# Output projection as seven half-size products instead of eight, in a hybrid encoder layer on one Trainium2 core

## The chip, the core and the metric

The kernel runs on one core of one Trainium2 chip. The metric is the device time of one execution in microseconds (us): the median of several runs of the whole program. The engines are called PE (TensorE, matrix products), PEld (its weight loads), DVE (VectorE), ACT (ScalarE), POOL (GpSimd) and SP (SyncE, which here only issues DMAs). POOL issues DMAs too, the stores above all.

## The reference, cut to what matters

One layer of an encoder on 1024 tokens of width 1024, in float32. Around the change it computes

```
merged = sigmoid(gate_a) * a_out + sigmoid(gate_b) * b_out
x  = x + gt1 * (merged @ w_o)                    # the output projection, w_o is 1024 x 1024
h2 = rmsnorm(x, norm2_g) * (1 + sc2) + sh2
f_gate, f_up = split(h2 @ w_ffn_in, 2)           # 2 x 2816 columns
x  = x + gt2 * ((silu(f_gate) * f_up) @ w_ffn_out)
```

`gt1`, `sc2` and `sh2` come from `mod = silu(c) @ w_ada + b_ada`, one column of 128 numbers at a time (48 columns).

## The kernel before, in words

Channels lie on the 128 partitions, tokens on the free axis; the tokens are worked in two halves of 512 ("half 0" and "half 1"). Every float32 operand is split into a high part (rounded to fp32r by ACT: `A.copy`) and a low part (`source - high`, on DVE: `V.tensor_tensor`), and a product is three matmuls: high x high, high x low, low x high (`mm3`, line 161; `multiply`, line 1286). Weights come as **units** of 128x1024: a DMA into a `raw` tile, ACT's cast to `wh`, DVE's difference to `wl` (`unit`, line 153). The three tags `raw`, `wh` and `wl` have three buffers each (pool `wpool`), and a load, a cast or a difference waits until the user of the unit three places earlier is done with that buffer. Tiles with the tag `mid` (128x2048) have eight buffers.

The program runs through these stages: `half(0)` and then `half(1)` (line 568), each with the input projections of query, key and value, the attention, the spatial gating, and at its end a loop over eight row blocks `d` that projects both branches (`w_ab`); `gate_products` (line 1295), the gates of row blocks 2 to 7 for both halves, already as seven products by Strassen's form; `out_projection(0)` and `out_projection(1)` (line 1395); then the feed-forward part (from line 1466), again by Strassen's form.

`out_projection(hf)` goes over eight row blocks `d` of the output. Each has one unit of `w_o`, 24 matmuls of 128x512 (eight `k`, three each) into one PSUM bank, then on DVE `x1 = bank * gt1 + x`, on ACT the square, on DVE the running sum of squares, and a store of `x1` to DRAM (`x1d`). The unit of `d + 2` is prepared beside `d`. In half 0, eight columns of `mod` (`ada_next`) and the split of half 1's merged rows run beside it; in half 1, the second norm of half 0 (`second_norm`: one DVE instruction, one of ACT, one of DVE for each of eight row blocks) does.

The loop over `d` at the end of `half(0)` (from line 1070) prepares the unit of `w_ab` for `d + 2`, computes the sum of squares of half 1's tokens, four columns of `mod` (`ada_next(2)` at `d` 2 and 3: each a raw load of 512 KB and a DVE instruction over 128x1024), and from `d` 5 on half 1's normalised input. In the first stage of `half(1)`, `ada_load` at `k` 0 to 5 loads twelve more columns, two to a `mid` tile, and `ada_late` uses them.

What sets the order: inside these stages `in_order[0]` is true, and then every DVE, ACT and PE instruction stays in the order of the program text (`Engine`, line 69), each engine working through its list and waiting at the head of it. Outside them a scheduler places instructions when the program is built. Loads on SP's queue (`load`) always keep program order, so that one which waits for a buffer holds all that come behind it. `in_order` is true in the loop at the end of `half(0)` in part only, and in `gate_products` throughout.

Of the kernel before, what the change touches and what calls it, by code (L numbers as in the profile page):

```python
# [8 lines left out]
F32 = mybir.dt.float32  # L9
F32R = mybir.dt.float32r  # L10
# [6 lines left out]
P = 128  # L17
# [24 lines left out]
def kernel(  # L42
# [58 lines left out]
    def nm(s):  # L101
        n_names[0] += 1
        return f"{s}_{n_names[0]}"
# [44 lines left out]
    def raw_unit(src):  # L148
        r = wpool.tile([P, UNIT], F32, tag="raw", name=nm("raw"))
        load(r, src)  # L150
        return r
# [94 lines left out]
    wS = dram.tile([NP, P, 4 * HALF], F32, tag="wS", name="wS")  # L246
    tA = dram.tile([NP, P, 4 * HALF], F32, tag="tA", name="tA")
    tB = dram.tile([NP, P, 4 * HALF], F32, tag="tB", name="tB")


    apool_ctx = ExitStack()
# [250 lines left out]
    def open_ffn():  # L502

        apool_ctx.close()
        fp = ffn_ctx.enter_context(pool("ffn"))
        fps.append(fp)
        for part in range(2):
            t = fp.tile([P, 2048], F32R, tag=f"b22{'hl'[part]}", name=nm("first"))
            firsts[part] = t

    def first_unit(i):

        r = raw_unit(w_gate[EARLY - 2 + i])
        h, l = (firsts[p][:, i * UNIT : (i + 1) * UNIT] for p in range(2))
        A.copy(h, r)
        V.tensor_tensor(l, r, h.bitcast(F32), op=ALU.subtract)
        return h, l

    halo_v = {}
    x1B = []  # L520
# [8 lines left out]
    def ada_late(r, col, row):  # L529

        V.scalar_tensor_tensor(out=r, in0=r, scalar=1.0, in1=row, op0=ALU.mult, op1=ALU.mult,
                               accum_out=acc_mod[:, col : col + 1])
        if col % 4 == 3:
            b = slice(col - 3, col + 1)
            if col < SH2:
                V.scalar_tensor_tensor(out=mod[:, b], in0=acc_mod[:, b], scalar=0.5, in1=base[:, b],
                                       op0=ALU.mult, op1=ALU.add)
            elif SC2 <= col < GT2:
                V.tensor_tensor(mod[:, b], acc_mod[:, b], g2c[:, col - SC2 - 3 : col - SC2 + 1], op=ALU.mult)
                V.tensor_tensor(mod[:, b], mod[:, b], base[:, b], op=ALU.add)  # L540
            else:
                V.tensor_tensor(mod[:, b], acc_mod[:, b], bada[:, b], op=ALU.add)
# [25 lines left out]
    def half(hf):  # L568
# [103 lines left out]
        for k in range(KT):  # L672
# [96 lines left out]
            if hf == 1:  # L769

                if k in (0, 2, 4):
                    wq_raw = raw_unit(w_q[k // 2 + 1])
                if k == 2:
                    wk_raw = raw_unit(w_kv[1])
                if k == 4:
                    wk = unit(None, V, wk_raw)
                if k in (1, 3, 5):
                    wq_next = unit(None, V, wq_raw)
                for _ in range((0, 0, 2, 2, 2, 3, 3, 0)[k]):
                    ada_late(*ada_loaded.pop(0), silu_c)  # L780
                if k < 6:
                    ada_load()
            sts = [(hH[k // 4][:, k % 4, t * P : (t + 1) * P], hL[k // 4][:, k % 4, t * P : (t + 1) * P])
# [286 lines left out]
        for d in range(KT):  # L1070
# [62 lines left out]
                    in_order[0] = False  # L1133
            if d == 4:
                h_next.extend([[hid(), hid()], [hid(), hid()]])
            if d in (2, 3):
                ada_next(2)
            if d > 4:
                for k in ((0, 1), (2, 3, 4), (5, 6, 7))[d - 5]:
                    xk = xs[k // 4][:, k % 4, :]  # L1140
                    hi, lo = (t[k // 4][:, k % 4, :] for t in h_next)
                    modulate(xk, rb, k, SC1, SH1, hi, lo, xk)
                    store(hd[1, k * P : (k + 1) * P, :], xk)
# [91 lines left out]
    def run_tokens(n):  # L1235
        for _ in range(n):
            if tokens:
                tokens.pop(0)()
# [56 lines left out]
    def gate_products(hH, hL):  # L1295
# [21 lines left out]
        for d in GD:  # L1317
            banks = {}
            for i, (u, part, t, b, first) in enumerate(STEPS):
# [30 lines left out]
                elif i == 6:  # L1350
# [4 lines left out]
                        split(merged[0][1][:, 3, :], mH[1][:, 3, :], mL[1][:, 3, :])  # L1355
                    gate_low(d + 1, 1)
                run_tokens((0, 4, 4, 4, 0, 0, 0)[i])
                if d == KT - 1:
                    if i == 2:
                        mH, mL = [hid(), hid()], [hid(), hid()]  # L1360
                    if i in (2, 3, 5):
                        for k in ((0, 1), (2, 3, 4), (), (5, 6))[i - 2]:
                            split(merged[0][k // 4][:, k % 4, :], mH[k // 4][:, k % 4, :],
                                  mL[k // 4][:, k % 4, :])
                    if i == 4:
                        wo_units.append(unit(w_o[0]))
                    if i == 6:
                        wo_units.append(unit(w_o[1]))
                if (d, i) == (GD[0], 5):
                    for hf in range(2):  # L1370
                        merged.append([midt(F32, 4), midt(F32, 4)])
# [12 lines left out]
                elif i == 6:  # L1384
# [2 lines left out]
                    merge(c21, ps[1, 1])  # L1387
                    V.tensor_tensor(merged[1][d // 4][:, d % 4, :], s, c21, op=ALU.add)
                    ps = load_p(d + 1)
        in_order[0] = False  # L1390
        return (mH, mL), merged[1]

    wo_units = []

    def out_projection(hf, m, m_next):

        mH, mL = m
        if hf == 1:
            h2[0] = [[hid(), hid()], [hid(), hid()]]
            dst = h2[0]  # L1400
            x1B.extend([midt(F32, 4), midt(F32, 4)])
            h2m.extend([midt(F32, 4), midt(F32, 4)])
        else:
            out = [[midt(F32R, 4), midt(F32R, 4)] for _ in range(2)]
            cond = midt(F32, 2)[:, 0, :]
            load(cond, cd)
        ss = ss_tile()[:, :HALF]

        def second_norm(k):
            xk = stream("hs")  # L1410
            load(xk, x1d[k * P : (k + 1) * P, :HALF])
            hi, lo = (t[k // 4][:, k % 4, :] for t in dst)
            modulate(xk, rb, k, SC2, SH2, hi, lo, h2m[k // 4][:, k % 4, :])

        for d in range(KT):
            wo = wo_units.pop(0)
            if d + 2 < KT:
                wo_units.append(unit(w_o[d + 2]))
            elif hf == 0:
                wo_units.append(unit(w_o[d + 2 - KT]))  # L1420
            elif d == KT - 1:
                raw1 = raw_unit(w_gate[1])
                raw2.append(raw_unit(w_gate[2]))
            if hf == 1 and d == 6:
                early.append(unit(w_gate[0], V))
            in_order[0] = hf == 0 and d < 2 or hf == 1 and d > 5
            if hf == 1 and d in (2, 5):
                early.append(first_unit(d // 3))
            xr = stream("xs")
            load(xr, x_rows(hf, d))  # L1430
            pw = mm_bank()
            for k in range(KT):
                kc = slice(k * P, (k + 1) * P)
                mm3(pw, (wo[0][:, kc], wo[1][:, kc]),
                    (mH[k // 4][:, k % 4, :], mL[k // 4][:, k % 4, :]), k == 0, k == KT - 1)
            if hf == 1:
                if d == 0:
                    col_rstd(sums[0], NT, rcol[2])
                elif d == 1:
                    rb = spread(rcol[2], NT)  # L1440
                for k in ((), (0,), (1, 2), (3,), (4, 5), (6,), (7,), ())[d]:
                    second_norm(k)
            else:
                ada_next((0, 0, 2, 2, 2, 2, 0, 0)[d], cond)
                split(m_next[d // 4][:, d % 4, :], out[0][d // 4][:, d % 4, :],
                      out[1][d // 4][:, d % 4, :])
            x1 = tmp() if hf == 0 else x1B[d // 4][:, d % 4, :]
            V.scalar_tensor_tensor(out=x1, in0=pw, scalar=mod[:, GT1 + d : GT1 + d + 1], in1=xr,
                                   op0=ALU.mult, op1=ALU.add)
            sumsq(x1, d == 0, ss)  # L1450
            store(x1d[d * P : (d + 1) * P, hf * HALF : (hf + 1) * HALF], x1)
            if hf == 1 and d == KT - 1:
                early.append(unit(None, V, raw1))
        in_order[0] = False
        sums.append(ss)
        if hf == 0:
            return out

    half(0)
    m = gate_products(*half(1))  # L1460
    m = out_projection(0, *m)
    out_projection(1, m, None)

    fp = fps[0]

    B11, B21 = ((h2[0][0][q], h2[0][1][q]) for q in range(2))
    T1, T2 = ((fpt(f"{n}h"), fpt(f"{n}l")) for n in ("tt1", "tt2"))


    RG, RU, U = {}, {}, {}
# [172 lines left out]
    def chain_rest():  # L1645
        def new_block(name):
            BLK[name] = (midt(F32R, 4), midt(F32R, 4))

        BLK["B22"] = (fpt("b22h"), fpt("b22l"))
        for name, q in (("T3", 0), ("T4", 1)):  # L1650
            for k in range(4):
                chain.append(lambda k=k, q=q, name=name: (k or new_block(name), t34_sum(q, k)))
                if k:
                    chain.append(lambda k=k, q=q, name=name:
                                 low(h2m[q][:, k - 1, :], BLK[name], k - 1))
            chain.append(lambda q=q, name=name: low(h2m[q][:, 3, :], BLK[name], 3))
# [342 lines left out]
```

## Time and profile before

| what | value |
| --- | --- |
| device time, median of 3 runs (lowest, highest) | 1227.25 us (1225.9, 1227.33) |
| span of the profiled execution, first to last instruction | 1224.2 us |
| device time outside that span, median less span | 3.05 us |
| PE busy in the span, matmuls | 1217.5 us (99%), 5701 |
| DVE, ACT, POOL busy | 897.4, 578.5, 148.7 us |
| granted TensorE clock | 1.000 |

The profiled execution's own device time is not listed; its span and the 3.05 us stand for it. A busy time is the union of an engine's instructions, which overlap a little where they follow each other; a row of the time line gives start, duration, engine, operation and tiles, and in brackets the idle time before it with what ended it.

### The profile page before, as it was taken

What the parts mean: (1) busy time and instruction counts of PE and PEld (TensorE: products, weight loads), DVE (VectorE), ACT (ScalarE), POOL (GpSimd) and SP (SyncE); (2) the same over time, 40 slices, a digit from 0 to 9 for tenths busy, and PEclk for the clock granted to TensorE, in tenths of its full rate; (3) what the DMA queues carried; (4) which work ended last, traced back from release to release, by engine and by line L of the source; (5) the groups of instructions that cost most, each with busy time, mean ns of one, the idle gap of its engine ahead of it and who ended that gap; (6) DMA issues with size and microseconds to landing.
All of it is one profiled execution on the core that took longest, in us unless ns stands there. A gap on an engine that the chain in (4) does not pass through costs nothing.

```text
span 1224.2 us, 15630 instructions
## 1 busy us (share of the span) xinstructions
PE 1217.5 (99%) x5701; PEld 1016.0 (83%) x5701; DVE 897.4 (73%) x1449; ACT 578.5 (47%) x944; POOL 148.7 (12%) x178
## 2 busy tenths in 40 slices
PE   9999999999999999999999999999999999999998
PEld 7888888888888888888888888888888888888887
DVE  9988877788878766877797766675676766765646
ACT  5667855367855434634453233333333334433341
POOL 0124323114331000011000001000000000010001
PEclk9999999999999999999999999999999999999999
DMA  9721179521176333597413446455555439995552
GB/s 366 283 86 52 35 241 361 223 86 53 35 276 222 120 104 121 198 322 264 154 52 120 172 155 224 172 176 202 189 189 187 167 153 367 393 364 190 189 172 104
DMA packets 75937, 230.79 MB, mean 189 GB/s; under 512 B 8658, under 2 KB 8914, under 8 KB 71124
## 3 DMA queue, kind: packets, MB, share of 16 engines
q1 hardware_dynamic: 61444, 161.62, 38.3%
q0 software_dynamic: 14416, 68.17, 14.9%
q8 instruction: 45, 0.74, 0.3%
q14 instruction: 32, 0.26, 0.1%
HBM read 174.70 MB, written 55.05 MB: 188 GB/s over the span
## 4 chain that ended last, share of the span: by engine, by line
PE 92%; DMA 4%; DVE 2%; issue 1%; ACT 1%; SPq 0%; POOL 0%; POOLq 0%; DVEq 0%; ACTq 0%
PE mm L79 48%; PE at L79 45%; DMA wS<-wo 1%; DMA mid<-in_w_ada_dram 1%; DMA raw<-in_w_q_dram 1%; DMA wo<-in_w_out_dram 1%; DMA mid<-in_xA_dram 0%; DVE mid L79 0%; ACT mid L79 0%; DVE wl L79 0%; DVE ws L79 0%; ACT wh L79 0%; DVE lb L79 0%; DVE hid L79 0%; DVE wo L79 0%
## 5 line engine op out<-in xcount | busy, mean ns | idle before, releaser
L79 PE MATMUL mm<-mid,wh 128*128 128x512 f32 x704 | 217.4, 390 | 0.0
L79 ACT CAST wh<-raw 128x1024 fp32r<-128x1024 f32 (+1 forms) x151 | 154.3, 1023 | 120.9 <-PE mm L79 45.6
L79 DVE TENSOR_TENSOR wl<-raw,wh 128x1024 fp32r<-128x1024 f32 (+1 forms) x137 | 161.5, 1183 | 62.1 <-ACT wh L79 61.1
L79 PEld LDWEIGHTS mm<-mid,wh 128*128 128x128 f32 x704 | 131.7, 188 | 27.1
L79 PE MATMUL mm<-mid,wl 128*128 128x512 f32 x352 | 137.0, 389 | 0.0
L79 PE MATMUL mm<-wh,h 128*128 128x512 f32 x384 | 124.6, 396 | 0.2 <-ACT h L79 0.2
L79 PE MATMUL mm<-h,wh 128*128 128x512 f32 x400 | 123.9, 391 | 0.0
L79 PEld LDWEIGHTS mm<-h,wh 128*128 128x128 f32 x400 | 74.6, 188 | 15.4
L79 PE MATMUL at<-h,wh 128*128 128x512 f32 x272 | 84.0, 390 | 0.0
L79 PEld LDWEIGHTS mm<-wh,h 128*128 128x128 f32 x384 | 70.8, 188 | 13.8 <-ACT h L79 0.4
L79 DVE TENSOR_TENSOR wl<-ws,wh 128x1024 fp32r<-128x1024 f32 (+1 forms) x54 | 60.7, 1125 | 24.5 <-ACT wh L79 24.5
L79 PE MATMUL mm<-h,wl 128*128 128x512 f32 x200 | 77.9, 389 | 0.0
L79 PEld LDWEIGHTS mm<-mid,wl 128*128 128x128 f32 x352 | 66.1, 188 | 13.8
L79 ACT CAST wh<-ws 128x1024 fp32r<-128x1024 f32 (+1 forms) x54 | 52.5, 973 | 42.3 <-DVE ws L79 27.4
L79 PE MATMUL mm<-wl,h 128*128 128x512 f32 x192 | 71.2, 391 | 0.0
L79 ACT ACTIVATE t<-t 128x512 f32<-128x512 f32 x53 | 32.8, 630 | 72.0 <-DVE t L79 71.9
L79 PEld LDWEIGHTS at<-h,wh 128*128 128x128 f32 x272 | 50.9, 188 | 10.5
L79 DVE TENSOR_TENSOR ol<-raw,oh 128x1024 fp32r<-128x1024 f32 x30 | 36.5, 1223 | 30.0 <-ACT oh L79 28.4
L79 ACT ACTIVATE xs<-xs 128x512 f32<-128x512 f32 x21 | 13.3, 633 | 94.0 <-DVE xs L79 94.0
L79 PE MATMUL at<-h,wl 128*128 128x512 f32 x136 | 53.1, 390 | 0.3 <-DVE wl L79 0.3
L79 PE MATMUL at<-wl,wh 128*128 128x512 f32 (+1 forms) x136 | 52.7, 388 | 0.0
L79 PE MATMUL at<-wh 128*128 128x512 f32 (+1 forms) x136 | 52.7, 387 | 0.0
(275 smaller groups left out, 2729.5 us busy)
## 6 DMA issues: line engine op xcount, KB each, us to landing
raw<-in_w_gate_dram SPq DMA_DIRECT2D x28, 512.0 KB, 3.8
tA<-hid POOLq DMA_DIRECT2D x11, 1024.0 KB, 4.6
tB<-hid POOLq DMA_DIRECT2D x11, 1024.0 KB, 5.0
wo<-in_w_out_dram POOLq DMA_DIRECT2D x22, 512.0 KB, 5.9
wS<-wo POOLq DMA_DIRECT2D x11, 1024.0 KB, 5.2
raw<-wS SPq DMA_DIRECT2D x44, 256.0 KB, 3.5
raw<-tB SPq DMA_DIRECT2D x44, 256.0 KB, 4.8
mid<-in_w_ada_dram SPq DMA_DIRECT2D x20, 512.0 KB, 9.8
```

The lines of the kernel that those rows point to most:

```text
L79: ins = f(*args, **kw)
```

## The change

The output projection of both halves is made by one level of Strassen's form (in Winograd's variant): row blocks are taken in four pairs, each pair needs seven products of 12 matmuls (four `k`, three each) instead of eight (two row blocks, two halves, two halves of `k`).

- **Weights.** Four of the seven products use sums of quarters of `w_o`. Those sums are made from `w_o` by `merged_sums(p)`: two loads of 512 KB into a `mid` tile, four DVE additions of 128x512, one store of 1 MB to a new DRAM tensor `sO`. Pairs 0 to 2 are made in the loop at the end of `half(0)`, pair 3 in the first stage of `half(1)`. The projection loads them back as units ("A", "C"); "0" and "B" are units of `w_o` itself. There are 14 units instead of 16.
- **Tokens.** The blocks T1 to T4 are sums of the merged rows of both halves: T1's four subtractions run in `gate_products` at `d` 4 and 5, its splits at `d` 7 (steps 4 and 5); T2, T3, T4 and the split of B22 are in a list `todo`, of which `run(3)` takes three entries after each product.
- **Order.** First the eight products of half 0's even row blocks (M1, M2), then for two pairs at a time T2, T3, T4, then T1 and B22. Each product is followed by its DVE addition into the rows it belongs to (`accumulate`, 28 instead of 16). The M1 bank stays open for T2, T3 and T4: each of these products continues in the bank that the addition before it has read.
- **Columns of `mod`.** The eight columns that `out_projection(0)` computed are moved ahead: `ada_next(2)` now runs at `d` 1 to 4 of `half(0)`, `ada_load` also at `d` 6 and 7, and `half(1)` uses sixteen instead of twelve.
- The second norm of half 0 is now in place in `h2m` and runs beside the last eight products; two tiles of the feed-forward part change places (`tt2`, `b22`).

The core of the diff:

```diff
+    sO = dram.tile([KT // 2, P, 4 * HALF], F32, tag="sO", name="sO")
...
+    def merged_sums(p):
+        t = mid.tile([P, 2048], F32, tag="mid", name=nm("wo"))
+        for i in range(2):
+            load(t[:, i * UNIT : (i + 1) * UNIT], w_o[2 * p + i])
+        a11, a12, a21, a22 = (t[:, i * HALF : (i + 1) * HALF] for i in range(4))
+        ops = [(a22, a21, a22), (a21, a11, a21), (a11, a22, a11), (a12, a11, a12)]
+        def one(n):
+            out, a, b = ops[n]
+            V.tensor_tensor(out, a, b, op=ALU.add)
+            if n == 3:
+                store(sO[p], t)
+        return one
...
-                for _ in range((0, 0, 2, 2, 2, 3, 3, 0)[k]):
+                for _ in range((0, 2, 2, 3, 3, 3, 3, 0)[k]):
                     ada_late(*ada_loaded.pop(0), silu_c)
+                if k == 2:
+                    sums3 = merged_sums(3)
+                if k > 3:
+                    sums3(k - 4)
...
-            if d in (2, 3):
+            if d in (1, 2, 3, 4):
                 ada_next(2)
+            if d > 5:
+                ada_load()
+            if d in (0, 2, 4):
+                pair_sums = merged_sums(d // 2)
+            if d < 6:
+                for n in range(2):
+                    pair_sums(2 * (d % 2) + n)
...
+                if d in (4, 5) and i in (1, 3):
+                    k = 2 * (d - 4) + i // 2
+                    o = merged[1][0][:, k, :]
+                    V.tensor_tensor(o, merged[0][0][:, k, :], o, op=ALU.subtract)
...
                     if i == 4:
+                        oblk["T1"] = (fpt("tt1h"), fpt("tt1l"))
                         wo_units.append(unit(w_o[0]))
+                    if i in (4, 5):
+                        for k in (2 * (i - 4), 2 * (i - 4) + 1):
+                            split(merged[1][0][:, k, :], *(t[:, k, :] for t in oblk["T1"]))
                     if i == 6:
-                        wo_units.append(unit(w_o[1]))
+                        wo_units.append(unit(w_o[2]))
...
+        first = [(0, "M1"), (1, "M1"), (2, "M1"), (0, "M2"), (3, "M1"), (1, "M2"), (2, "M2"), (3, "M2")]
+        for n, (p, name) in enumerate(first):
+            product(p, name)
+            if n == 0:
+                make("0", 2)
+                fetch("0", 3)
+            if n == 3:
+                make("0", 3)
+                fetch("A", 0)
+            if n == 5:
+                make("A", 0)
...
+            accumulate(c11[p], banks[p, "a" if name == "M1" else "b"], gt, 2 * p)
+            if name == "M2":
+                square(c11[p], 0, 2 * p)
+            run(3)
...
+        second = [(p, name) for q in (0, 2) for name in ("T2", "T3", "T4") for p in (q, q + 1)]
+        for n, (p, name) in enumerate(second):
+            product(p, name)
...
+            if name == "T2":
+                accumulate(row(1, 2 * p), e, gt, 2 * p)
+            elif name == "T3":
+                accumulate(row(1, 2 * p + 1), e, ngt, 2 * p + 1)
+            else:
+                accumulate(row(0, 2 * p + 1), e, ngt, 2 * p + 1)
+                square(row(0, 2 * p + 1), 0, 2 * p + 1)
+            run(3)
...
+        third = [(p, name) for q in (0, 2) for name in ("T1", "B22") for p in (q, q + 1)]
+        for n, (p, name) in enumerate(third):
+            product(p, name)
...
+            for k in ((), (0,), (1, 2), (3,), (4,), (5,), (6, 7), ())[n]:
+                second_norm(k)
...
     half(0)
-    m = gate_products(*half(1))
-    m = out_projection(0, *m)
-    out_projection(1, m, None)
+    out_products(gate_products(*half(1)))
```

More of the change, by code (lines that the diff above doesn't have):

```diff
@@ L506, in open_ffn, with first_unit @@
         fps.append(fp)
[L507 to L513, printed above, removed]
+    def first_unit(i, r):
         h, l = (firsts[p][:, i * UNIT : (i + 1) * UNIT] for p in range(2))
@@ L1389, in gate_products @@
                     ps = load_p(d + 1)
-        in_order[0] = False
[L1391 to L1457, printed above, removed]
@@ L1459 @@
     half(0)
-    m = gate_products(*half(1))
-    m = out_projection(0, *m)
-    out_projection(1, m, None)
+    out_products(gate_products(*half(1)))
     fp = fps[0]
     B11, B21 = ((h2[0][0][q], h2[0][1][q]) for q in range(2))
-    T1, T2 = ((fpt(f"{n}h"), fpt(f"{n}l")) for n in ("tt1", "tt2"))
+    T1, T2 = ((fpt(f"{n}h"), fpt(f"{n}l")) for n in ("tt1", "b22"))
     RG, RU, U = {}, {}, {}
@@ L1647, in new_block @@
             BLK[name] = (midt(F32R, 4), midt(F32R, 4))
-        BLK["B22"] = (fpt("b22h"), fpt("b22l"))
+        BLK["B22"] = (fpt("tt2h"), fpt("tt2l"))
         for name, q in (("T3", 0), ("T4", 1)):
```

180 lines of the change are left out of this document (added).

## The prediction, made before the changed kernel ran

> **What bounds the kernel now.** I read the engines' share and the 40 slices first, then the chain of waits, then a table of stretches (span, busy time of each engine, clock, share of the DMA engines, GB/s).
>
> ```profile
> PE 1217.5 (99%) x5701; PEld 1016.0 (83%) x5701; DVE 897.4 (73%) x1449; ACT 578.5 (47%) x944; POOL 148.7 (12%) x178
> DVE  9988877788878766877797766675676766765646
> DMA  9721179521176333597413446455555439995552
> ```
> ```profile
> 459.46 5.44 PE mm L79 x24
> ...
> 497.54 51.68 PE mm L79 x228
> ```
> ```profile
> core 0: us, PE busy (x) PEld busy (x) DVE busy (x) ACT busy (x) POOL busy (x), PEclk, DMA share, GB/s
> 161.00:206.70 45.70, 45.70 (x212) 37.85 (x210) 35.16 (x51) 24.90 (x38) 13.47 (x23) 1.00 0.85 300
> 206.70:237.25 30.55, 30.55 (x170) 26.60 (x168) 21.41 (x37) 6.47 (x8) 0.87 (x2) 1.00 0.75 294
> ...
> 500.10:545.00 44.90, 44.90 (x200) 37.18 (x199) 37.98 (x56) 19.43 (x27) 3.95 (x8) 1.00 0.83 284
> 545.00:588.90 43.90, 43.90 (x203) 36.60 (x202) 30.91 (x40) 18.30 (x24) 5.63 (x9) 1.00 0.77 258
> ```
>
> PE is busy without a break, at the full clock, and ends the chain; a 128x512 matmul takes 5.44 / 24 = 0.2267 us from start to start. Fewer matmuls are therefore worth their time, as long as their operands come in time. The four stretches are the two that the change loads (the end of half 0 with the first stage of half 1, 161 to 237.25) and the two output projections (500.1 to 588.9). There DVE is busy 0.70 to 0.85 of the time, and the DMA engines 0.75 to 0.85: both are close behind PE.
>
> **The change, part by part.** *Matmuls:* 28 products of 12 instead of 32 take away 48 x 0.2267 = 10.9 us.
>
> *Prices on DVE and ACT.* DVE's instructions overlap where they follow each other, so I take the spacing.
>
> ```profile
> 504.05 1.23 DVE L79 TENSOR_TENSOR wl<-raw,wh 128x1024 fp32r<-128x1024 f32 x1 [0.26 <-ACT wh L79]
> 505.19 0.69 DVE L79 SCALAR_TENSOR_TENSOR t<-t,xs 128x512 f32<-128x512 f32 x1
> ...
> 508.80 2.49 DVE L79 TENSOR_TENSOR mid<-mid,mid 128x512 fp32r<-128x512 f32 x4
> ```
> ```profile
> 580.30 0.75 DVE L79 SCALAR_TENSOR_TENSOR h<-mid,mod,h 128x512 fp32r<-128x512 f32 x1 [0.79 <-ACT h L79]
> 580.97 0.74 DVE L79 SCALAR_TENSOR_TENSOR mid<-mm,mod,xs 128x512 f32<-128x512 f32 x1
> ...
> 587.07 0.69 DVE L79 TENSOR_TENSOR ss<-ss,t 128x512 f32<-128x512 f32 x1 [0.76 <-ACT t L79]
> ```
> ```profile
> 505.35 2.18 ACT L79 CAST mid<-mid 128x512 fp32r<-128x512 f32 x4
> ...
> 590.60 1.99 ACT L79 CAST wh<-raw 128x1024 fp32r<-128x1024 f32 x2
> ```
>
> A low part or sum over 128x512 takes DVE (2.49 - 0.69) / 3 = 0.60; an addition from PSUM with a column factor 0.67 (580.30 to 580.97); a unit's low part 1.14 (504.05 to 505.19). ACT's cast takes 0.55 over 512 columns and 0.95 over 1024. When DVE needs at once what ACT makes from its last result (square, then sum; modulate), it stands idle for 0.76 to 0.79. In program order nothing behind can fill that time; this is the point on which I differ from a count of busy time.
>
> ```profile
> 500.10 0.62 PE L79 MATMUL mm<-h,wh 128*128 128x512 f32 x2
> ...
> 505.54 0.62 PE L79 MATMUL mm<-h,wh 128*128 128x512 f32 x2
> 505.99 0.39 PE L79 MATMUL mm<-h,wl 128*128 128x512 f32 x1
> ```
> *(1) The second product waits.* Product (1, M1) uses `w_o[2]`, prepared where `w_o[1]` was. Its low part was ready at 504.05 + 1.23 = 505.28, which was early enough: its first product began at 505.54, and its low was read at 505.99. Now the unit is due after 12 matmuls: its low at 500.10 + 14 x 0.2267 = 503.27. That is 2.0 late as it stands. The splits of T1 (four casts, four lows) lie ahead of it in both queues: + 4 x 0.60 = 2.4, so 4.4. Between 0 (T1's splits in idle time, and the unit made sooner) and 4.4 I take 4.4, because cast and low both stand behind work that waits for the last gate products.
>
> *(2) The fifth product waits.* `wh` has three buffers, and the unit of (3, M1) takes that of `w_o[0]`, which is in use to the end of the fourth product. The fifth product is next on PE. The least is the cast, 0.95, and the low, 1.2, less the two matmuls that need no low, 0.45: 1.8. DVE has in front of it the last rows of the gate, three additions of 0.67 and nine `todo` entries of 0.60 since 507.7; ACT has nine entries. I take 5.1, the upper end.
>
> *(3) The first T3 waits.* It goes on in the bank that the addition after the first T2 must have read. Between `w_o[2]`'s low (507.7) and the end of that addition DVE has 30 entries of 0.60 (18.1), five units of 1.14 (5.7) and nine additions of 0.67 (6.0): 29.8. Idle come three squares (3 x 0.77) and about 4.5 for units whose cast can start only when a product frees its `wh` buffer. That is 36.6 and ends at 544.3. PE, with (1), (2) and 0.4 on the third product (its unit's low comes straight behind), comes there at 500.1 + 10 x 2.72 + 9.9 = 537.2. The wait is 7.1; without the idle time it would be 0.3. Both ends stay.
>
> *(4) The middle.* The twelve products of `second` are 32.6 us; DVE has 20.7 us of entries and some 10 of idle: about 1.2 lost.
>
> *(5) The end.* Eight products (21.8), and beside them what stood beside the 43.9 us of the second projection: eight modulates (16 x 0.66 = 10.6), seven additions (4.7), seven sums of squares (4.2), four units (4.6): 24.1, and idle 7 x 0.77 + 8 x 0.79 + units 1.2 + 1.6 at its start = 14.5. DVE needs 38.6 and ends about 613; PE would need its eight products, the column sums and the first 21 matmuls of the feed-forward, 27.4. The 12.7 too late falls as 7.5 and 1.5 on the last two B22 (their bank waits for the addition of T1, which stands behind the modulates) and 3.7 inside the second product of the feed-forward part, which reads rows 6 and 7. The column sums of half 1 then wait 1.6 more. From below: with the idle time filled, nothing is late.
>
> ```profile
> 594.46 0.95 PE L79 MATMUL at<-ones,ss 128*128 128x1 f32 x8
> ```
> Sum (1) to (5): 4.4 + 0.4 + 5.1 + 7.1 + 1.2 + 7.5 + 1.5 + 3.7 + 1.6 = 32.5. Without waits those column sums would come at 500.1 + 336 x 0.2267 + 0.9 (two small steps) + 24 x 0.2267 = 582.6, which is 11.9 before 594.46 (10.9 of matmuls, 1.0 of small waits). So 582.6 + 32.5 = 615.1: **20.7 us later**; between -6 (only 5 of waits) and +21.
>
> *(6) The end of half 0 and the first stage of half 1.* Added there: eight loads of `w_o` (4.2 MB), three stores of 1 MB (3.1; the fourth falls behind it), four raw columns (2.1), four columns into `mid` (2.1): 11.5 MB.
>
> ```profile
> GB/s 277 311 373 346 193 0 62 213 211 337 352 400 273 284 408 185 316 331 305 340 415 423 417 419 417 417 421 410 415 421 417 415 413 370 251 131 165 0 0 32
> DMA packets 6615, 22.66 MB, mean 297 GB/s; under 512 B 849, under 2 KB 849, under 8 KB 6608
> ...
> raw<-in_w_ab_dram SPq DMA_DIRECT2D x4, 512.0 KB, 5.3
> ```
> These are the same 76.25 us in 40 slices; where the DMA engines are full, they move 417 GB/s. 22.66 + 11.5 = 34.2 MB take 82 us at that rate: + 6. At the rate per busy share of the two stretches, 22.7 MB in (0.85 x 45.7 + 0.75 x 30.55) = 61.8 us, 0.367 MB per us, it is 93: + 17. On DVE come twelve sums (7.2) and four raw columns of 1.23 (4.9): 35.2 + 12.1 = 47.3 in 45.7 us, + 1.6 at least.
>
> ```profile
> 171.21 1.23 DVE L79 TENSOR_TENSOR wl<-raw,wh 128x1024 fp32r<-128x1024 f32 x1 [0.25 <-ACT wh L79]
> ...
> 185.48 1.23 DVE L79 SCALAR_TENSOR_TENSOR raw<-raw,silu_c 128x1024 f32<-128x1024 f32 x1 [1.57 <-DMA raw<-in_w_ada_dram]
> ```
> DVE waited for a column there already. From `d` 1 to 4 three loads of 512 KB share three `raw` buffers, where only `d` 2 and 3 had three; SP's queue holds the next `w_ab` and `w_q` units behind them, and a unit ahead on DVE stands behind sums that wait for loads. The waits fall on `d` 4 to 7 and on `k` 4. I take 14, nearer the upper end because the order of the queue can't use what is left free; 0 and 26 are the ends (all covered; DMAs 15% slower than now).
>
> *At nothing:* the loads of the projection itself (14 units of 512 KB for 16, each fetched a product or more before its cast), `ngt` (0.08), the stores of `x1`, the exchange of `tt2` and `b22`. What covers the loads is the free quarter of the DMA engines there (0.83 and 0.77); without it one that comes too late costs up to its landing time, 5.3 us in the row above.
>
> **The sum:** 1224.2 + 14 + 20.7 + 3.05 = 1262 us, against 1227.25.
>
> **The rivals.** *R1, faster:* DVE isn't the bound, because at the table's 0.77 (68.9 us in 88.8) it has 20 us of idle time, and 73 us of the new work fit beside 76.2 us of products if order allows it. Only the ring of `wh` then costs, (2), 1.8 to 5.1, and the stage of half 0 is covered: 1227.25 - 10.9 + 3.5 = 1220. Against it: rows 580.30 and 587.07, idle time that program order leaves. It decides where DVE reaches the first T2 addition before 537.
>
> *R2:* the loads of half 0 are covered (0 to 3) and only the projection waits: 1227.25 + 20.7 = 1248. For it: the slices of 0 and 62 GB/s near 171; against it: row 185.48.
>
> *R3:* the waits also cost the clock. At the start of the program the first matmuls are slow:
>
> ```profile
> 1.86 4.24 PE L79 MATMUL at<-zeros 128*128 128x512 f32 x10 [1.86 <-DVE identr L79]
> 5.99 1.95 PE L79 MATMUL at<-crow,ident 128*128 128x512 f32 x4
> ```
> Ten in 4.24 and four in 1.95 are 6.2 us for what takes 14 x 0.2267 = 3.2 later: up to 3 us after each long wait. With four to six of (1), (2), (3), (5) and (6) long enough, it is 1262 + 11 = 1273. Nothing else in before can show it: PE is busy 99%, and the clock is 1.00 in every stretch. The Trainium skill, "TensorE: Matmul & The Clock Gate", Part 1: The HAM clock gate, says that the clock halves after an idle window of about 3.4 us and returns after as long a busy one; by it the waits of 4.4, 5.1, 7.1 and 7.5 would each be followed by about 1.7 us of loss (an estimate), 7 together, and 1269.
>
> *R4, no change:* the waits cancel the matmuls, 8 to 14 in all with half 0 covered: 1227.
>
> **How the numbers follow.** The forecast, 1262, has 0.45, with its own range of 1250 to 1270; R2 0.22 (1236 to 1250); R3 0.17 (1270 to 1284); R1 0.12 (1216 to 1224); R4 0.04. The range of 8 in 10, 1236 to 1280, takes the first two and most of R3. A difference of 0.2% (2.5 us) is about what a measurement of this kernel can tell from none. Faster by more: R1, 0.12; within: R4, 0.04; slower: the rest, 0.84.
>
> **What would show it.** In the trace of the changed kernel: an idle PE, ended by ACT or DVE `wh`, `wl`, ahead of the second (about 4.4) and the fifth product (5.1); one ended by DVE `mm` ahead of the first T3 (7.1), and DVE above 0.8 busy with idle ended by ACT `t` and `h`; the column sums of half 1 some 115 us behind the first product with `w_o`, instead of 94; in the loop of half 0, PE waits from `d` 4 on, ended by DVE `wl`, with the DMA share near 1.0, and half 1's attention some 14 late. It would be wrong if PE runs through both stages without breaks (R1), if half 0's stage is dense (R2), or if the granted clock falls behind the waits (R3).

## The result and the profile after

The changed kernel takes 1288.99 us (median of 4 runs, 1286.6 to 1290.2) against 1227.29 us: a ratio of 1.0504, 95% interval 1.0489 to 1.0518, 61.7 us slower. The direction was forecast, the size was not: 1262 was the forecast, 1280 the end of the range. The profiled execution has a span of 1288.2 us. All runs of one kernel here and below lie within 0.4% of each other, but for one of the ten of `e12_before_512`: it took 4373 us, for a reason that no trace shows, and is left out of that kernel's ratio.

The page of the changed kernel, its shares and slices:

```profile
PE 1241.3 (96%) x5653; PEld 1015.4 (79%) x5653; DVE 932.1 (72%) x1505; ACT 584.2 (45%) x955; POOL 150.7 (12%) x182
...
PE   9999997899999999779799999999999999999998
...
PEclk9999997999999999989989999999999999999999
```

PE has 48 matmuls fewer and is busy 23.8 us longer. A slice is 32.2 us. PE has holes in two places, slice 7 (193 to 225 us, at half 0's end) and slices 17, 18 and 20 (515 to 644 us, the projection); the granted clock drops in slices 7, 18 and 21. The same in the table of stretches (span, busy time of PE, PEld, DVE, ACT, POOL, clock, DMA share, GB/s):

```profile
core 0: us, PE busy (x) PEld busy (x) DVE busy (x) ACT busy (x) POOL busy (x), PEclk, DMA share, GB/s
161.00:185.00 24.00, 23.14 (x107) 18.87 (x106) 16.81 (x27) 9.21 (x15) 5.03 (x6) 1.00 0.78 277
185.00:206.00 21.00, 16.01 (x68) 12.78 (x68) 15.49 (x24) 7.87 (x14) 6.33 (x10) 0.84 0.91 347
206.00:264.00 58.00, 48.88 (x226) 39.15 (x226) 46.55 (x76) 17.75 (x28) 6.44 (x12) 0.94 0.93 364
527.00:552.00 25.00, 18.08 (x63) 12.97 (x62) 19.31 (x30) 10.60 (x16) 0.56 (x1) 0.86 0.37 123
552.00:601.00 49.00, 41.02 (x168) 32.11 (x166) 34.31 (x45) 17.76 (x23) 2.72 (x5) 0.93 0.62 209
601.00:648.00 47.00, 37.74 (x149) 26.59 (x150) 30.50 (x42) 17.91 (x25) 6.47 (x11) 0.92 0.40 144
```

PE's time line of the changed kernel has the forecast waits nearly one by one; in brackets the idle time and what ended it:

```profile
524.24 0.73 PE L79 MATMUL mm<-mid,wh 128*128 128x512 f32 x2 [0.69 <-DVE t L79]
...
532.36 0.73 PE L79 MATMUL mm<-h,wh 128*128 128x512 f32 x2 [2.36 <-ACT wh L79]
533.62 0.50 PE L79 MATMUL mm<-h,wl 128*128 128x512 f32 x1 [0.52 <-DVE wl L79]
...
545.92 1.22 PE L79 MATMUL mm<-h,wh 128*128 128x512 f32 x2 [3.84 <-ACT wh L79]
```
```profile
572.35 1.22 PE L79 MATMUL mm<-mid,wh 128*128 128x512 f32 x2 [6.58 <-DVE mid L79]
```
```profile
642.62 1.58 PE L79 MATMUL at<-h,wh 128*128 128x512 f32 x2 [4.48 <-ACT h L79]
...
647.80 1.84 PE L79 MATMUL at<-ones,ss 128*128 128x1 f32 x8 [0.98 <-DVE ss L79]
```

Added up from the starts of the matmuls (time to the next start beyond 0.227 us, waits over 0.3 us):

| place | forecast | measured |
| --- | --- | --- |
| (1) second product, with the last gate product ahead of it | 4.4 | 0.9 + 3.5 = 4.4 |
| (2) fifth product | 5.1 | 4.4 |
| (3) first T3 | 7.1 | 6.8 |
| (4) middle | 1.2 | 2.1 |
| (5) last products to the column sums | 14.3 | 13.1 |
| (6) half 0's end and half 1's first stage | 14 | 23 |

Row (6) is the delay of one and the same matmul of half 1, behind the stage, before and after:

```profile
262.18 0.39 PE L79 MATMUL mm<-wl,h 128*128 128x512 f32 x1
```
```profile
286.16 0.40 PE L79 MATMUL mm<-wl,h 128*128 128x512 f32 x1
```

That is 24.0, less the 0.9 by which the second profile is late ahead of the stage already; "the attention is late" below is this delay, worked out in the same way.

Rows (1) to (5) agree. Yet half 1's column sums come 120.7 us after the first product with `w_o` (527.12 to 647.80), not 115, and from there to the end the kernel takes 640.4 us, where the kernel before took 629.7 for the same 2770 matmuls. So three things were missing in the sum: part of (6), something that slows PE between the waits, and something behind the projection.

### The profile page after: what moved, and what is told of

Its sections match the earlier page's. It is cut to its first block, busy times and chain, and to the rows that moved or that the text cites. A ratio compares the mean times of both kernels' runs of the same rounds, so it can differ in the third digit from the quotient of the medians.

```text
span 1288.2 us, 15633 instructions
## 1 busy us (share of the span) xinstructions
PE 1241.3 (96%) x5653; PEld 1015.4 (79%) x5653; DVE 932.1 (72%) x1505; ACT 584.2 (45%) x955; POOL 150.7 (12%) x182
## 4 chain that ended last, share of the span: by engine, by line
PE 52%; DVE 2%; ACT 1%; issue 0%; DMA 0%; SPq 0%; ACTq 0%; DVEq 0%
PE at L79 33%; PE mm L79 19%; DVE mid L79 1%; ACT wh L79 0%; DMA raw<-sO 0%; DVE h L79 0%; ACT h L79 0%; DVE wl L79 0%; DVE ss L79 0%; ACT t L79 0%; DVE first L79 0%; ACT first L79 0%; SPq L131 0%; ACTq L79 0%; DVEq L79 0%
## 5 line engine op out<-in xcount | busy, mean ns | idle before, releaser
L79 PE MATMUL mm<-mid,wh 128*128 128x512 f32 x640 | 203.7, 400 | 13.5 <-DVE mid L79 8.2
L79 PEld LDWEIGHTS mm<-mid,wh 128*128 128x128 f32 x640 | 121.9, 192 | 42.9 <-DVE mid L79 9.2
L79 PE MATMUL mm<-mid,wl 128*128 128x512 f32 x320 | 126.2, 396 | 0.6 <-DVE wl L79 0.5
L79 PE MATMUL at<-h,wh 128*128 128x512 f32 x304 | 99.0, 404 | 7.6 <-ACT h L79 6.3
L79 PE MATMUL mm<-h,wh 128*128 128x512 f32 x304 | 96.4, 399 | 6.2 <-ACT wh L79 6.2
L79 PEld LDWEIGHTS at<-h,wh 128*128 128x128 f32 x304 | 58.6, 194 | 23.7 <-ACT h L79 8.4
L79 PEld LDWEIGHTS mm<-h,wh 128*128 128x128 f32 x304 | 57.5, 191 | 18.9 <-ACT wh L79 7.0
L79 PE MATMUL mm<-h,wl 128*128 128x512 f32 x152 | 60.7, 399 | 0.7 <-DVE wl L79 0.7
L79 PE MATMUL at<-h,wl 128*128 128x512 f32 x152 | 60.5, 398 | 0.5 <-DVE wl L79 0.5
L79 ACT COPY t<-mm 128x512 f32<-128x512 f32 x48 | 27.9, 585 | 61.2 <-PE mm L79 44.8
```

Of the source, the lines that this page charges most:

```text
L79: ins = f(*args, **kw)
```

## The experiments

Theory after these views: four causes, which add up. (a) The load on half 0 costs 23 us. (b) The waits of the projection are DVE's order and the `wh` ring, as forecast. (c) After a wait PE runs at half clock. (d) Tiles have moved in memory, and the matmuls that read them are slower. Rivals: for (a), DVE's order or the transfers; for (b), DVE's plain amount of work; for (c), want of operands; for (d), traffic, or the tiles' new roles. Shown below are the edits against the changed kernel unless said otherwise. Times of one group were taken on one chip beside runs of the kernel before, with medians of 1226.3, 1226.6 and 1226.8.

**The address: `e1_pad`, `e2_before_shift`, `e5_pad128`, `e9_place`, `e12_before_512`.** The same 901 matmuls of the feed-forward part in before, in the changed kernel and in `e9_place`, no wait in any:

```profile
626.96:831.00 204.04, 204.04 (x901) 168.92 (x900) 145.80 (x204) 75.28 (x108) 13.95 (x26) 1.00 0.46 165
```
```profile
683.58:891.46 207.88, 207.88 (x901) 168.84 (x900) 145.56 (x203) 75.14 (x107) 13.93 (x26) 1.00 0.45 163
```
```profile
680.16:884.19 204.03, 204.03 (x902) 168.87 (x900) 145.78 (x204) 75.16 (x108) 13.94 (x26) 1.00 0.46 165
```

The clock is 1.00 in all three, the other engines do the same work, and the middle one is 3.8 us longer. From start to start, the matmuls that read a `tt1`, `tt2` or `b22` tile take 226.7 ns before and 233.5 in the changed kernel. The new tile `ngt`, 32 bytes, lies ahead of those tiles in memory: the first of them starts at address 175424 before and at 175456 in the changed kernel, and the others are moved by the same 32 bytes.

```diff
# e1_pad (e5_pad128: 4 * KT)
-        ngt = small.tile([P, KT], F32, tag="ngt1", name="ngt1", bufs=1)
+        ngt = small.tile([P, 2 * KT], F32, tag="ngt1", name="ngt1", bufs=1)[:, :KT]
# e9_place
+        ngt = acc_mod[:, GT1 : GT1 + KT]
# e2_before_shift, in the kernel before (e12_before_512: 128 columns)
+        space = small.tile([P, KT], F32, tag="space", name="space", bufs=1)
+        G.memset(space, 0.0)
```

> The changed kernel with the tile of the negated columns, ngt, made 16 columns wide instead of 8 (64 bytes instead of 32 on each partition); nothing else. In the changed kernel 1152 matmuls that read a tt1, tt2 or b22 tile came 233.5 ns apart, not 226.7; those tiles had moved by 32 bytes, to addresses that no longer are multiples of 64. Theory: the address alone does it; here they are back at 226.7 and the kernel is 8 to 12 us faster than the changed one, 1277 to 1281. Rival: the spacing comes from something else that differs (the clock, other traffic): no change, 1289.

Measured 1284.04 us, ratio 1.0469 (1.0454 to 1.0485): about half of what was expected. These matmuls took 229.8 ns.

> The kernel before with a tile of 32 bytes that nothing reads, put at the same place in memory. Theory (address): its 1008 matmuls that read tt1, tt2 or b22 take 233.5 ns each, + 7 us, 1234 to 1238. Rival: no change, 1227.

Measured 1236.12 us, ratio 1.0082 (1.0067 to 1.0097). One unused tile of 32 bytes makes the kernel before 9.8 us slower. The 1008 matmuls at 6.8 ns are 6.9 us of it; the rest is spread over others, `mm<-mid,wh` above all (226.9 to 228.3 ns from start to start). Two groups of the moved matmuls, and two of the kernel before; the number behind the comma is the mean duration of one in ns:

```profile
L79 PE MATMUL at<-b22h,wh 128*128 128x512 f32 x84 | 33.3, 396 | 0.0
L79 PE MATMUL at<-b22h,wl 128*128 128x512 f32 x84 | 33.2, 396 | 0.0
```
```profile
L79 PE MATMUL at<-tt1h,wh 128*128 128x512 f32 x85 | 33.2, 391 | 0.0
...
L79 PE MATMUL at<-b22h,wh 128*128 128x512 f32 x84 | 32.7, 389 | 0.0
```

> As e1_pad, with the tile made 32 columns wide: 128 bytes. e1_pad had the tiles at multiples of 64 again (of 128 too, where before had them 64 past one), and its tt1, tt2 and b22 matmuls came 229.8 ns apart, between 226.7 and 233.5. Theory: the place within 128 bytes matters; here it is that of before, and these matmuls are back at 226.7: 1277 to 1280. Rival: what is left in e1_pad comes from the changed roles of the tiles or other traffic: as e1_pad, 1282 to 1285.

Measured 1284.84 us, ratio 1.0475 (1.0458 to 1.0493): the theory of 128 bytes fell, 232.8 ns.

> The changed kernel with the negated columns ngt put into columns of acc_mod that are no longer needed, so that no memory is taken and every tile behind it lies where it lay before; nothing else. In e1_pad (64 bytes) and e5_pad128 (128) the tt1, tt2 and b22 matmuls stayed at 229.8 and 232.8 ns. Theory: any shift of these tiles against the other operands costs, and only the old addresses give 226.7: the matmuls are back at it, 8 to 12 us faster than the changed kernel, 1277 to 1281. Rival: the tiles' new roles or the traffic slow them: 1284, as e5_pad128.

Measured 1278.86 us, ratio 1.0426 (1.041 to 1.0441); 226.8 ns. Neither roles nor traffic are to blame: `ngt` cost some 10 us by its place (1288.99 to 1278.86, ratios 1.0504 and 1.0426).

> The kernel before with a tile of 512 bytes that nothing reads in the place where e2_before_shift had 32. Every operand of the matmuls lies at one and the same place within 512 bytes in the kernel before, and does so again here. Theory C (only the place within 512 bytes counts): no change, 1226 to 1228. Theory D (any shift of the tiles against the others costs): 1231 to 1236.

Measured 1227.25 us, ratio 1.0001 (0.9991 to 1.0011); 226.7 ns. Shifts of 0 and 512 bytes cost nothing, 32, 64 and 128 cost 6.8, 3.1 and 6.1 ns a matmul. In the kernel before, `wh`, `wl`, `h`, `mid` and these tiles all start 320 bytes past a multiple of 512. Theory C stands for the shifts tried. Why it is so (which two accesses get in each other's way) was not tried.

**Half 0: `e3_no_sums`, `e4_no_columns`, `e6_sums_later`, `e10_additions_only`.**

```diff
# e3_no_sums (with e1_pad): no merged_sums in half 0 and half 1, and in fetch
-                    load(r[:, j * HALF : (j + 1) * HALF],
-                         sO[p][:, (2 * j + i) * HALF : (2 * j + i + 1) * HALF])
+                    load(r[:, j * HALF : (j + 1) * HALF], w_o[2 * p + j][:, i * HALF : (i + 1) * HALF])
# e4_no_columns (with e1_pad): the places of before; the last eight columns stay zero
-            if d in (1, 2, 3, 4):
+            if d in (2, 3):
                 ada_next(2)
-            if d > 5:
-                ada_load()
...
# e6_sums_later (with e5_pad128): pair_sums one d later
+            if 0 < d < 7:
+                for n in range(2):
+                    pair_sums(2 * ((d - 1) % 2) + n)
...
-            if d < 6:
-                for n in range(2):
-                    pair_sums(2 * (d % 2) + n)
# e10_additions_only (with e9_place): the additions stay, no load and no store; fetch as in e3_no_sums
-            load(t[:, i * UNIT : (i + 1) * UNIT], w_o[2 * p + i])
+            if i:
+                G.memset(t, 0.0)
...
-            if n == 3:
-                store(sO[p], t)
```

> As e1_pad, with the sums of w_o left out of half 0 and of half 1's first stage (no loads, additions or stores of them); the projection loads quarters of w_o in place of the sums, the same bytes, so it multiplies by other numbers. The eight columns of mod stay moved. The delay of half 1's attention against before was 24 us. Theory A (the sums themselves, DVE standing still for their loads): 18 to 22 us faster than e1_pad, about 1260. Theory B (the DMA engines are full, 34.5 MB): 7.3 MB less leave 27.2, all of the delay goes, about 1256. Here the two differ little; e4_no_columns is the other half.

Measured 1268.86 us, 15.2 less than `e1_pad`; half 1's attention is 6.7 us later than before instead of 23. Less than either theory had.

> As e1_pad, with the sums, but the columns of mod computed where the kernel before computed them and the last eight (the shift of the second norm) left out and taken as zero. Theory A (DVE stands still for the loads of the sums): only 4 to 10 us faster than e1_pad, about 1274. Theory B (bytes): 4.2 MB less leave 30.3 MB, which 76 us can carry at 400 GB/s: nearly all of the delay goes, about 1258.

Measured 1274.35 us, 9.7 less than `e1_pad`. Theory B, as I had put it, falls: 30.3 MB did not fit. At its upper end theory A fits the time; whether its mechanism does, the next run asks.

> As e5_pad128, with each of the additions for pairs 0 to 2 one step of d later, so that DVE comes to them when their loads have landed (in the changed kernel it stood 2.27 and 1.49 us for them, and ms, on which PE's column sums hang, stood behind). Theory A (waits in DVE's order): 5 to 8 us faster than e5_pad128. Rival B (DMA engines full, raw buffers late): within 2 us of it.

Measured 1285.31 us against 1284.84: nothing. DVE's waits for `w_o` are 1.21 and 0.24 us, where `e5_pad128` has 1.71 and 1.76 (the changed kernel 2.27 and 1.49), and PE still has waits of 3.7, 3.1 and 2.3 in the stage. Theory A falls, and its fit to the time of `e4_no_columns` was luck.

> As e9_place, with the sums' sixteen additions on DVE in their places, but without their loads and stores: they add tiles that GpSimd has cleared, and the projection loads quarters of w_o (the same bytes) in place of the sums. Theory B' (after e6_sums_later changed nothing: the transfers are the delay, since the DMA engines move 400 to 420 GB/s without a break): the delay of the attention falls from 23 to 7 to 10 us, that of e3_no_sums, 12 to 16 us faster than e9_place. Theory A' (DVE's extra work): at most 4 us faster.

Measured 1265.73 us, 13.1 less than `e9_place`: with all of the additions on DVE, and only the transfers gone, nearly the whole gain of `e3_no_sums` is there. The attention is 10 us late, some 3 more than in `e3_no_sums`, where the additions are gone too. So it is the transfers above all, though without the free room that theory B gave them: taking away 7.3 MB saves 13.1 to 15.2 us and 4.2 MB 9.7, that is 1.8 to 2.3 us per MB, and a MB at 417 GB/s takes 2.4. Some room was used: where only the 4.2 MB of columns are added (`e3_no_sums`), the attention is 6.7 us late, and where only the sums are (`e4_no_columns`), 12.3, that is 1.6 to 1.7 us per MB. The edit takes the loads of `w_o` out of SP's queue together with their bytes; whether the bytes count, or the place that they take in the queue ahead of other loads, was not told apart. The transfers of the stage, in the changed kernel (161 to 264) and in `e10_additions_only` (161 to 262), in 40 slices:

```profile
GB/s 252 352 408 425 177 0 255 256 358 388 415 410 415 161 262 379 333 372 393 420 415 425 415 444 280 366 407 414 426 407 418 410 410 409 410 407 402 53 0 255
DMA packets 9632, 35.04 MB, mean 340 GB/s; under 512 B 1184, under 2 KB 1184, under 8 KB 9225
```
```profile
GB/s 335 408 297 107 0 208 219 274 385 415 261 260 373 232 324 333 305 419 422 414 422 410 417 414 423 417 412 410 407 412 312 178 0 0 201 32 182 105 102 0
DMA packets 8202, 28.40 MB, mean 281 GB/s; under 512 B 1025, under 2 KB 1025, under 8 KB 8195
```

In the first, the engines stand above 400 from slice 20 to 37 but for two, some 41 us. The free slices near 175 us don't take that work: SP's queue issues its loads in order and stands there from 165.4 to 177.2, its longest wait in the stage (what waited, what ended it, total, number, longest):

```profile
SPq L131 <- PE mm L79: 11.7, 1, 11.7
```

**The clock: `e7_warm`.** After a long wait the matmuls start 0.43 us apart; here behind the wait for a unit of `w_ab` in the changed kernel:

```profile
214.83 2.08 PE L79 MATMUL mm<-mid,wh 128*128 128x512 f32 x4 [3.75 <-ACT wh L79]
216.70 0.63 PE L79 MATMUL mm<-mid,wl 128*128 128x512 f32 x1
217.13 1.05 PE L79 MATMUL mm<-mid,wh 128*128 128x512 f32 x2
...
221.18 0.61 PE L79 MATMUL mm<-mid,wh 128*128 128x512 f32 x2
```

From 216.70 to 217.13 is one matmul; from 221.18 on they are 0.227 apart. The Trainium skill, "TensorE: Matmul & The Clock Gate", Part 1: The HAM clock gate, has half the clock until PE has been busy for some 3.4 us, and says that the window runs freely; the trace agrees in kind, not in the time: here and behind the wait of 3.84 us the clock is full again only 6.1 us after PE has started.

```diff
# e7_warm (with e5_pad128); ahead of product(p, name) in first, and likewise 26 in second
+        def warm(bank, w, t, count):
+            for k in range(count):
+                T.matmul(bank, w[0][:, :P], t[0][:, 0, :], start=True, stop=True)
...
+            if n in (1, 4):
+                banks[p, "a"] = mm_bank()
+                warm(banks[p, "a"], units["0", n // 4], oblk["B11"], 8 if n == 1 else 15)
```

> As e5_pad128, with matmuls of no use put into three of PE's waits of the projection: 8 ahead of (1, M1), 15 ahead of (3, M1), 26 ahead of the first T3 (1.8, 3.4 and 5.9 us at full clock, each less than the wait that it stands in), into banks that the next use overwrites. Theory (after an idle PE the clock is halved): the 24 matmuls that took 0.43 us instead of 0.23 after these waits are gone, 4 to 5.5 us faster than e5_pad128. Rival (they are slow for want of operands or from traffic): no change.

Measured 1281.78 us, 3.1 less than `e5_pad128`, somewhat under the 4 expected. As a time this is hardly clear of the noise (four runs of 1280.71 to 1285.67, against 1283.7 to 1285.85); what shows the clock is the trace. Its time line at the fifth product:

```profile
540.35 3.56 PE L79 MATMUL mm<-h,wh 128*128 128x512 f32 x15
544.40 0.73 PE L79 MATMUL mm<-h,wh 128*128 128x512 f32 x2 [0.49 <-ACT wh L79]
545.65 0.50 PE L79 MATMUL mm<-h,wl 128*128 128x512 f32 x1 [0.52 <-DVE wl L79]
545.99 0.63 PE L79 MATMUL mm<-h,wh 128*128 128x512 f32 x2
```

The product starts when its unit is there, as late as ever, but runs at full clock. In `e5_pad128` 19 matmuls behind these three waits were slow (3.8 us), here none. In the whole changed kernel there are 42 at 0.43 us behind waits, 8.4 us.

**DVE's order: `e8_fill`.**

```diff
# e8_fill (with e5_pad128), in square; modulate's low part likewise waits in a list, lows
+        def flush():
+            while pend:
+                s, q = pend.pop(0)
+                V.tensor_tensor(s, s, q, op=ALU.add)
...
                 A.activation(q, t, AF.Square)
-                V.tensor_tensor(sq[hf], sq[hf], q, op=ALU.add)
+                flush()
+                pend.append((sq[hf], q))
```

> As e5_pad128, with DVE's order in the projection changed so that it doesn't wait for ACT: the sum of squares is added one product later, and the low part of a normalised row after the next row's first instruction. The same instructions, nothing left out. Theory (DVE sets the pace, its idle time on ACT is some 11 us of it): the wait ahead of the first T3 falls from 6.6 to about 4, those of the last eight products by 7 to 8: 9 to 13 us faster than e5_pad128. Rival (DVE's busy time itself is the bound, or the wh buffers): 3 us or less.

Measured 1277.34 us, 7.5 less than `e5_pad128`: under the 9 to 13, well over the rival's 3. From the first T3 to half 1's column sums it takes 70.7 us in place of 75.3, 4.7 less where 7 to 8 were expected. The wait ahead of the first T3 is 3.56 us, and DVE ahead of it has no idle time on ACT's squares any more (before the edit three gaps of 0.70):

```profile
568.22 1.22 PE L79 MATMUL mm<-mid,wh 128*128 128x512 f32 x2 [3.56 <-DVE mid L79]
```
```profile
560.16 0.74 DVE L79 SCALAR_TENSOR_TENSOR xs<-at,mod,xs 128x512 f32<-128x512 f32 x1
560.82 0.68 DVE L79 TENSOR_TENSOR ss<-ss,t 128x512 f32<-128x512 f32 x1
561.42 1.89 DVE L79 TENSOR_TENSOR mid<-mid,mid 128x512 fp32r<-128x512 f32 x3
```

What is left there is work and units that wait for their buffer. So both were right in part: idle time in DVE's order, and DVE's amount of work.

**What is left: `e11_projection_alone`.** The edits of `e9_place`, `e3_no_sums`, `e4_no_columns`, `e8_fill` and `e7_warm` (12 in place of 26) together.

> As e9_place, with the whole load on half 0 taken away (the sums left out as in e3_no_sums, the eight columns left out as in e4_no_columns) and with the order of e8_fill and the matmuls of no use of e7_warm (8, 15 and 12). What is left is the projection by seven products, with its weights' sums for nothing and its cheaper order. Theory (its waits are more than the 10.9 us of matmuls): 1238 to 1246, slower than before's 1226.6 still. Rival (the projection is a gain, only half 0 loses): below 1225.

Measured 1243.48 us, ratio 1.0144 (1.0129 to 1.0159). Half 1's attention is 0.3 us late. So the projection by seven products loses by itself: the attention is on time, and half 1's column sums come 14.8 us later than before. PE's waits from 160 to 652 us, in total, number and longest:

```profile
PE at L79 <- DVE h L79: 4.5, 4, 2.3
PE at L79 <- DVE ss L79: 3.0, 3, 1.6
PE mm L79 <- DVE mid L79: 2.0, 4, 1.2
PE mm L79 <- DVE wl L79: 1.1, 2, 0.5
PE mm L79 <- ACT wh L79: 1.0, 2, 0.5
```

The matmuls of no use stand in the waits ahead of the second, fifth and first T3 product (8 + 15 + 12 of 0.227 us are 7.9 us); the column sums are 14.8 - 0.3 later although 10.9 us of matmuls are gone, so some 25 us of waiting are left in the projection, theirs included. Without their 7.9 us it would still be behind, 16.7 less 7.9. No version of these beats the kernel before, and none was tried that makes the sums elsewhere, since even with free sums it would stay behind.

## Why the prediction was wrong, step by step

**Matmuls, 10.9 us:** right; 48 fewer, and where PE has its operands, they start 0.227 us apart.

**(1) to (5), the waits of the projection:** right in place and releaser, and 30.8 us in all for 32.5. `e8_fill` shows the mechanism for (3) and (5). No run tried (1), (2) and (4) by themselves. In (5) the prediction spread 12.7 us over the last products, though its own 38.6 and 27.4 are 11.2 apart; (5) measured 13.1 in all for 14.3. For (2) I named the `wh` ring and took the upper end for what stands ahead in the queues. Both are in it, as ACT's time line shows:

```profile
544.31 0.62 ACT L79 CAST mid<-mid 128x512 fp32r<-128x512 f32 x1 [1.85 <-DVE mid L79]
544.83 1.04 ACT L79 CAST wh<-raw 128x1024 fp32r<-128x1024 f32 x1
```

The buffer is free when the fourth product ends, at 542.1. The unit's cast starts 2.7 us later, behind a cast of T3 that waits for its sum from DVE; the rest is the cast itself and the unit's low part.

**(6), half 0:** the first term that was mis-sized: 14, measured 23 (inside its ends, 0 and 26). The step that failed is "22.66 + 11.5 = 34.2 MB take 82 us at that rate: + 6". The bytes were right, 34.5 MB, but it spread them over the 76 us, free slices included. `e3_no_sums`, `e4_no_columns` and `e10_additions_only` show that nearly every MB came on top, at 1.6 to 2.3 us where the full rate is 2.4. Whether for want of bandwidth or by the order of the queue stays open. The view ahead of that sentence had it already: some 417 GB/s for 13 slices in a row. DVE's waits for `w_o`, which I named beside it, are real and worth nothing (`e6_sums_later`).

**R3, the clock:** wrongly set up as a rival. It does not stand in place of the waits but follows them, and belonged into the sum: 8.4 us, of which `e7_warm` took 3.1 back. The 11 that I gave it was near.

**At nothing, `ngt` (0.08):** the step that put the time outside the range's reach. As an instruction it does cost that; as a tile it cost some 10 us (`e9_place`), through matmuls in stages that the change does not touch. No row of before could show it, since there all of these tiles lay well. With the three, 1262 + 9 + 5.4 + 10 is 1286; the 23 of (6) hold 15 of the 42 slow matmuls already, so the clock adds 5.4 here. The last 3 us (4, since (1) to (5) came out 1.7 shorter than forecast) are not assigned; about 1 of them lies in the first 20 us of that profile, and varies from run to run.

**The rivals:** R1 (DVE has room) and R4 fell with the waits in the table; R2 (half 0 covered) with the 23 us. That `e11_projection_alone` is close to R2's 1248 says little: it has a cheaper order on DVE and matmuls of no use in three waits, and slow matmuls (11) only behind the column sums.

## What to carry to other kernels

Fewer matmuls pay only where DVE, ACT and the buffers can hand over operands at the new pace: put the work per product on each in-order engine beside the product's time, idle round trips included, and add the slow clock behind every wait of a few us. Added bytes in a stage whose transfers stand at the full rate for long can cost most of their time, whatever the mean share says. And a small new tile can move everything allocated behind it: compare the addresses, not only the instructions.

## What the runs showed of the hardware that was not expected

A matmul of 128x512 that reads its moving operand from a tile shifted by 32, 64 or 128 bytes against the other operands starts the next 233.5, 229.8 or 232.8 ns later, not 226.7; by 512 bytes, no difference. The clock went down behind waits shorter than expected too: in `e9_place` six matmuls ran at 0.43 us behind the second product's wait of some 2.5 us; in the changed kernel's profile, behind the same wait, none did.
